# Block-diagonal products of a chunked recurrence over the whole systolic array, two lanes at a time, and attention values two key tiles at a time

## The chip, the cores and the metric

One core of a Trainium2 chip. The metric is the device time of one execution in microseconds (us); the time before is the median of three timed runs, 4041.27 us (4037.69 to 4042.21). A profile is one further execution. PE is the matrix engine (PEld its weight loads), DVE the vector engine, ACT the scalar engine, POOL the general engine, and SP the engine that issues the DMAs spoken of here.

## The reference, cut to what matters

Two trunk layers run over 1024 latent and 256 context tokens of width 1024. Layer 0 mixes the tokens with a bidirectional recurrence over 16 heads, each with a 64 x 64 state; layer 1 with attention of 16 query heads over 4 key and value heads. Each layer ends in a squared-ReLU MLP.

```python
def _wkv_step(state, inp):
    r, w, k, v, kk, bvec = inp
    sa = jnp.einsum('bhvk,bhk->bhv', state, -kk)
    state = state * w[:, :, None, :] + sa[..., None] * bvec[:, :, None, :] + v[..., None] * k[:, :, None, :]
    y = jnp.einsum('bhvk,bhk->bhv', state, r)
    return state, y
...
        sc = jnp.einsum('bqkgd,bskd->bkgqs', q, k_all) * scale
        p = jax.nn.softmax(sc, -1)
        return jnp.einsum('bkgqs,bskd->bqkgd', p, v_all)
```

## The kernel before, in words

The kernel is one program of stages: preparation of the recurrence, the recurrence itself (the chains), its readout and output projection, MLP 0, projections of queries, keys and values, attention, output projection, MLP 1. All in float32; a float32 product is two matmuls in the trace.

**The chains.** The recurrence is cut into chunks of 32 tokens, 40 of them, and runs forwards and backwards at once. Four lanes (`Chain`, one for each four heads: two channel tiles `ct2` by two heads `h`) each make 40 steps; a step serves one chunk in each direction `d`. A step has four stages:

- stage 0 (L859 to L863): eight products give the chunk's right-hand sides, 32 rows each, into `ps_x`, each in a quarter of the array's columns (`tile_position=(0, q)`); ACT copies them to `X`.
- stage 1 (L865 to L874): eight products with the chunk's inverse, again a quarter each, into the other half of `ps_x`; four copies, mostly ACT's, put the result into the stack `SV`. The inverse lies in `T`, for each quarter 32 columns that are zero outside the quarter's own rows; POOL makes it (`inverses`, L843) by multiplying with a mask, one step ahead.
- stage 2 (L879 to L885): eight products with `LS` give the next state, 64 rows for each head, each in a half of the array's columns, into `ps_s`; DVE multiplies by the decay into the next `SV`, twice.
- stage 3 (L887 to L895): eight products give the chunk's outputs, a quarter each, into `ps_y`; ACT copies (first visit of a chunk) or DVE adds (second) to `y`.

`ps_x` has three buffers, `ps_s` and `ps_y` two each. `staggered` (L918) calls the lanes in turn: a round of 16 turns gives each lane its four stages at turns 0, 5, 10 and 11 (`STAGES`), the lanes four turns apart. That is the order in which the instructions are written; a scheduler then places them on the engines by readiness and priority. `Lanes.load` (L800) sends the next two steps' operands, in up to 14 portions of a two-round period (`SENDS`): `ST` (weights of stages 0, 1 and 3), `LS` and the values in `SV`, each send held back until the matmul marked last (`L.mark`) has run. The early and late rounds also carry the first part of the readout (`Readout.center` and `scale`, on DVE, POOL and ACT) beside them.

**The attention** (`phase_e`, L1336). A unit is one head pair and 512 queries; it runs over ten key tiles. For each: four products of full width give the scores `ps_s` (L1404, L1405), ACT takes the exponential into `p`, POOL adds it to `acc` for the sums, and `values` (L1358) multiplies `p` with the value tile, two products of 64 columns each into the two halves of `ps_av`. `values` lags by `AVLAG` = 2 tiles; one tile's values are issued in each iteration. Between them stand products for the next heads' maxima (`ps_m`, L1241), and in the fourth iteration of a unit the sums of the unit before (`ps_su`, L1375), also of 64 columns. `line` ties all of them into one order on PE.

Of the kernel before, what the change touches and what calls it, by code (L numbers as in the profile page):

```python
# [774 lines left out]
class Lanes:  # L775


    def __init__(self, k, es):
        tc, nc = k.tc, k.nc
        sb = lambda n, b: es.enter_context(tc.tile_pool(name=n, reuse_waits="tile", bufs=b))  # L780
        ps = lambda n, b: es.enter_context(tc.tile_pool(name=n, reuse_waits="tile", bufs=b, space=PSUM))
        vp = sb("vp", 1)
        self.gp, self.xp = sb("gp", 2), sb("xp2", 2)
        self.bp = sb("bp", 1)
        self.px, self.pss, self.py = ps("px", 3), ps("pss", 2), ps("py", 2)
        self.SV = [vp.tile([128, 2, 2, 4, 4, 64], F32, name=f"SV{b}", tag=f"SV{b}") for b in range(2)]
        self.LS = [[vp.tile([128, 2, 2, 2, 2, 64, 2], F32, name=f"LS{lp}{b}", tag=f"LS{lp}{b}") for b in range(2)] for lp in range(2)]
        for b, a, h in itertools.product(range(2), range(2), range(2)):
            q = QUAD[a, h] * 32
            (nc.gpsimd if b else nc.vector).memset(self.SV[b][q:q + 32, h, a], 0.0)  # L790
        for h in range(2):
            nc.vector.memset(self.SV[0][h * 64:h * 64 + 64, h, :, 0:4:3], 0.0)
        for t in (self.LS[lp][b] for b in range(2) for lp in range(2)):
            for h in range(2):
                rows = slice(h * 64, h * 64 + 64)
                eye = k.c["ident"][rows, rows].unsqueeze(1).unsqueeze(3).to_broadcast([64, 8, 64, 2])
                nc.scalar.copy(t[rows, h].rearrange("p l d a e c -> p (l d a) e c"), eye)
        self.ST = {}

    def load(self, k, i, mark=None):  # L800

# [8 lines left out]
        for lp in range(2):  # L810
# [4 lines left out]
                yield  # L815
            for h in range(2):
                anti = slice(64 - h * 64, 128 - h * 64)
                send(LS[anti, h].rearrange("p l d a e c -> p (l d a e c)"), S["LS"][h, i, :, :, lp * 2:lp * 2 + 2].rearrange("b s l d a f e -> (b s) (l d a f e)"))
                yield
            for a in range(2) if lp == 0 else ():  # L820
                for h, d in itertools.product(range(2), range(2)):
# [3 lines left out]


class Chain:

# [14 lines left out]
    def step(self, s):  # L845
# [12 lines left out]
        xu = L.px.tile([128, 2, 2, 64], F32, name="ps_x", tag="xu")  # L858
        for ct2, h, d in units:  # L859
            q = QUAD[ct2, h] * 32  # L860
            L.mark = nc.tensor.matmul(xu[q:q + 32, 0, d, :], stack(ct2, h, d, 0), sv(h, ct2, d), start=True, stop=True, tile_position=(0, q))  # L861
        X = L.xp.tile([128, 2, 64], F32, name="X", tag=f"X{pr}")
        L.copied = nc.scalar.copy(X, xu[:, 0])  # L863
        yield
        for ct2, h, d in units:  # L865
            q = QUAD[ct2, h] * 32
            L.mark = nc.tensor.matmul(xu[q:q + 32, 1, d, :], T[:, d, q // 32, :], X[:, d, :], start=True, stop=True, tile_position=(0, q))  # L867
        lo, hi = sorted((2 * gf + c, 2 * gb + 1 - c))
        first = lo not in self.seen
        self.seen |= {lo, hi}  # L870
# [5 lines left out]
        if s + 1 < self.n:  # L876
            self.inverses(s + 1)
            i2, c2 = divmod(s + 1, 2)
            pst = L.pss.tile([128, 2, 2, 64], F32, name="ps_s", tag="s")  # L879
            for ct2, h, d in units:  # L880
                L.mark = nc.tensor.matmul(pst[h * 64:h * 64 + 64, ct2, d, :], ls[:, h, ln, d, ct2, :, c], sv(h, ct2, d), start=True, stop=True, tile_position=(0, h * 64))  # L881
            for h in range(2):
                rows = slice(h * 64, h * 64 + 64)
                pt = k.c["PT"][rows, pr * 2:pr * 2 + 2, :, s + 1].unsqueeze(3).to_broadcast([64, 2, 2, 64])
                nc.vector.tensor_tensor(L.SV[i2 % 2][rows, h, :, both(c2), pr, :], pst[rows], pt, ALU.mult)  # L885
        yield
        psy = L.py.tile([128, 2, 64], F32, name="ps_y", tag="y")  # L887
        for ct2, h, d in units:
            q = QUAD[ct2, h] * 32
            L.mark = nc.tensor.matmul(psy[q:q + 32, d ^ rev, :], stack(ct2, h, d, 32), sv(h, ct2, d), start=True, stop=True, tile_position=(0, q))  # L890
        o = self.y[:, lo:hi + 1:hi - lo, :]
        if first:
            nc.scalar.copy(o, psy)
# [17 lines left out]
                gens.remove(g)  # L911


STAGES = (0, 5, 10, 11)
SENDS = (2, 4, 6, 8, 9, 10, 12, 14, 16, 18, 20, 22, 23, 24)


def staggered(k, L, gens):  # L918


    sends = iter(())
    for t in range(16 * Chain.n + 16):
        i, at = divmod(t, 32)
        if at == 0 and i + 1 < len(Chain.seq):
            sends = L.load(k, i + 1, lambda: L.mark)
        for l, g in enumerate(gens):
            if t >= 4 * l and (t - 4 * l) % 16 in STAGES:
                next(g, None)
        if at in SENDS:
            next(sends, None)  # L930
        yield

# [403 lines left out]
def phase_e(k, outs, qs, qp, mp):  # L1336
# [5 lines left out]
    with ExitStack() as es:  # L1342
# [52 lines left out]
        for i, (ct, half) in enumerate(units):  # L1395
# [4 lines left out]
            for kt in range(10):  # L1400
# [18 lines left out]
                for part in range(2):  # L1419
                    at += 1  # L1420
                    while sent < min(at + MXLEAD, 2 * (at - MX0)):
                        next(mx, None)
                        sent += 1
                    next(post, None)
                    if part == 0 and len(late) > AVLAG:
                        values(*late.popleft())
            done = (ct, half), st
        while late:
            values(*late.popleft())
# [68 lines left out]
```

## Time and profile before

| | |
|---|---|
| median of the timed runs | 4041.27 us |
| the profiled execution's own time | 4029.49 us |
| span of its instructions | 4027.7 us |
| PE busy | 3598.4 us (89%) |
| DVE busy | 2199.1 us (55%) |
| ACT busy | 1507.4 us (37%) |
| POOL busy | 1478.4 us (37%) |
| first and last start of a chain product (L861, L890) | 1013.2, 1417.4 us |
| first and last start of a score product (L1404) | 2747.3, 3184.4 us |

In the rows of a profile, `out<-in` names the tiles, `128*32 128x64` means weights of 128 rows by 32 columns and an operand of 128 partitions by 64 elements. In a timeline, a row has start, duration of the merged group, engine, line and count, and in brackets the engine's idle time before and what ended it; "issue" means that nothing in the profile explains the wait. A matmul's duration overlaps that of its neighbours, so the pace is read from starts.

### The profile page before, as it was taken

The numbers are of one execution on the slowest core, as the hardware profiler recorded it, in microseconds if no ns is written. First come the engines' busy times: TensorE is split into PE (matmuls) and PEld (weight loads), VectorE is DVE, ScalarE is ACT, GpSimd is POOL, SyncE is SP. The second block draws the span as 40 slices with busy tenths as digits, with TensorE's granted clock in tenths as the row PEclk, the third lists the DMA queues.
The fourth block names the chain that finished last, engine by engine and source line by source line (L and its number), as shares of the span: only waits on it lengthen the run. The fifth ranks groups of instructions, "written<-read, shape, count | busy, mean of one in ns | idle before, by whom it ended". The sixth has DMA issues, their size and how long they took to land.

```text
span 4027.7 us, 70776 instructions
## 1 busy us (share of the span) xinstructions
PE 3598.4 (89%) x28100; PEld 2789.5 (69%) x28100; DVE 2199.1 (55%) x3707; ACT 1507.4 (37%) x3223; POOL 1478.4 (37%) x1387
## 2 busy tenths in 40 slices
PE   5999866885677779999999999899999999999998
PEld 3667655664566669788888888765444578888886
DVE  6337789988654784533333335567766453333334
ACT  5666555454455433322111113433444332212222
POOL 3114685665533533111111111135877512222221
PEclk7999965886898789999999999999999999999999
DMA  7456777677777543211111111432010111111111
GB/s 284 144 187 171 171 177 170 160 177 178 198 205 215 163 133 104 80 39 38 42 40 40 38 42 70 138 105 79 17 32 17 63 38 51 47 48 47 50 53 68
DMA packets 397562, 414.77 MB, mean 103 GB/s; under 512 B 152864, under 2 KB 282144, under 8 KB 397104
## 3 DMA queue, kind: packets, MB, share of 16 engines
q1 hardware_dynamic: 396272, 408.94, 36.0%
q8 instruction: 222, 3.64, 0.4%
q0 software_dynamic: 960, 1.31, 0.2%
q14 instruction: 108, 0.88, 0.1%
HBM read 294.99 MB, written 117.11 MB: 102 GB/s over the span
## 4 chain that ended last, share of the span: by engine, by line
PE 66%; DVE 11%; issue 4%; DMA 2%; ACT 1%; POOL 1%; SPq 1%; DVEq 0%; POOLq 0%; ACTq 0%
PE ps_pj L271 45%; PE ps_av L1364 4%; PE ps_s L881 2%; PE ps_m L1241 2%; PE ps_s L1404 2%; PE ps_pj L290 2%; PE ps_s L1405 2%; DVE Tn L713 1%; DVE To L712 1%; PE ps_y L890 1%; PE ps_x L861 1%; PE ps_x L867 1%; DVE sgw L630 1%; DVE KT L653 0%; DVE AR L647 0%
## 5 line engine op out<-in xcount | busy, mean ns | idle before, releaser
L255 POOL TENSOR_TENSOR w_lo<-w_raw,w_hi 128x512 fp32r<-128x512 f32 (+1 forms) x292 | 476.5, 1633 | 1682.5 <-ACT w_hi L253 1635.8
L271 PE MATMUL ps_pj<-xh,w_hi 128*128 128x512 f32 (+1 forms) x1712 | 627.5, 367 | 7.3 <-ACT w_hi L253 5.9
L271 PE MATMUL ps_pj<-xh,w_lo 128*128 128x512 f32 (+1 forms) x1712 | 618.6, 365 | 7.1 <-POOL w_lo L255 7.1
L271 PE MATMUL ps_pj<-xl,w_hi 128*128 128x512 f32 (+1 forms) x1712 | 623.1, 365 | 0.0
L1122 DVE SCALAR_TENSOR_TENSOR xr<-ps_pj,c_mod,xr 128x512 f32<-128x512 f32 (+1 forms) x368 | 251.8, 686 | 564.2 <-PE ps_pj L271 557.4
L253 ACT CAST w_hi<-w_raw 128x512 fp32r<-128x512 f32 (+1 forms) x292 | 216.3, 742 | 836.4 <-PE ps_pj L271 594.6
L271 PE MATMUL ps_pj<-hid_l,w_hi 128*128 128x512 f32 (+1 forms) x1280 | 474.4, 371 | 0.0
L271 PE MATMUL ps_pj<-hid_h,w_hi 128*128 128x512 f32 (+1 forms) x1280 | 473.1, 371 | 0.0
L271 PE MATMUL ps_pj<-hid_h,w_lo 128*128 128x512 f32 (+1 forms) x1280 | 469.8, 370 | 0.0
L1146 DVE TENSOR_TENSOR m_q<-m_r 128x512 f32<-128x512 f32 x160 | 183.8, 1150 | 416.9 <-ACT m_r L1144 416.5
L271 PEld LDWEIGHTS ps_pj<-xh,w_hi 128*128 128x128 f32 x1712 | 325.1, 190 | 62.7 <-ACT w_hi L253 7.9
L271 PEld LDWEIGHTS ps_pj<-xh,w_lo 128*128 128x128 f32 x1712 | 322.9, 190 | 61.2 <-POOL w_lo L255 10.0
L271 PEld LDWEIGHTS ps_pj<-xl,w_hi 128*128 128x128 f32 x1712 | 325.0, 190 | 52.2 <-issue 1.4
L1415 POOL TENSOR_TENSOR acc<-acc,p 128x1024 f32<-128x1024 f32 x122 | 294.8, 2416 | 60.8 <-ACT p L1408 56.6
L271 PEld LDWEIGHTS ps_pj<-hid_h,w_hi 128*128 128x128 f32 x1280 | 241.4, 189 | 44.2
L271 PEld LDWEIGHTS ps_pj<-hid_h,w_lo 128*128 128x128 f32 x1280 | 241.1, 188 | 43.7
L271 PEld LDWEIGHTS ps_pj<-hid_l,w_hi 128*128 128x128 f32 x1280 | 241.4, 189 | 43.3
L1408 ACT ACTIVATE p<-ps_s 128x1024 f32<-128x1024 f32 x160 | 163.5, 1023 | 229.4 <-PE ps_s L1405 229.4
L271 PE MATMUL ps_pj<-xhi,w_hi 128*128 128x512 f32 (+1 forms) x576 | 230.1, 408 | 16.3 <-ACT xhi L479 10.6
L271 PE MATMUL ps_pj<-xlo,w_hi 128*128 128x512 f32 (+1 forms) x576 | 228.2, 397 | 7.4 <-DVE xlo L480 7.2
L1245 DVE TENSOR_REDUCE mc<-ps_m 128x1 f32<-128x512 f32 x256 | 174.8, 690 | 99.8 <-PE ps_m L1241 96.1
L271 PE MATMUL ps_pj<-xhi,w_lo 128*128 128x512 f32 (+1 forms) x576 | 224.1, 391 | 5.5 <-POOL w_lo L255 5.5
(236 smaller groups left out, 6781.0 us busy)
## 6 DMA issues: line engine op xcount, KB each, us to landing
wmod<-in_wmod SPq DMA_DIRECT2D x32, 1024.0 KB
w_raw<-in_m SPq DMA_DIRECT2D x64, 512.0 KB
w_raw<-in_m SPq DMA_DIRECT2D x128, 256.0 KB
ST<-d_ST SPq DMA_DIRECT2D x80, 320.0 KB
d_ST<-AR SPq DMA_DIRECT2D x160, 128.0 KB
d_LS<-KT SPq DMA_DIRECT2D x320, 64.0 KB
d_ST<-G SPq DMA_DIRECT2D x160, 128.0 KB
ST<-d_ST SPq DMA_DIRECT2D x80, 256.0 KB
```

Of the source, the lines that this page charges most:

```text
L253: nc.scalar.copy(hi, raw)
L255: getattr(nc, eng).tensor_tensor(lo, raw, hi.bitcast(F32), ALU.subtract)
L271: i = nc.tensor.matmul(ps[:, :n], w[:, sl], x[:, t0:t0 + n], start=a, stop=z)
L290: nc.tensor.matmul(ps[:, :n], w[:, sl], x[:, t0:t0 + n], start=a, stop=z)
L881: L.mark = nc.tensor.matmul(pst[h * 64:h * 64 + 64, ct2, d, :], ls[:, h, ln, d, ct2, :, c], sv(h, ct2, d), start=True, stop=True, tile_pos ...
L1122: k.nc.vector.scalar_tensor_tensor(x[:, t0:t0 + n], ps[:, :n], g, x[:, t0:t0 + n], ALU.mult, ALU.add)
L1146: nc.vector.tensor_tensor(q[:, :n], r[:, :n], r[:, :n], ALU.mult)
L1241: line(nc.tensor.matmul(ps[:, o:o + n], Q[:, (t + i) * 128:(t + i) * 128 + 128], K_[:, t0:t0 + n], start=True, stop=True))
L1245: line(nc.vector.tensor_reduce(mc[:, t + u, t0 // 512:t0 // 512 + 1], ps, AX.X, ALU.max), "v")
L1364: line(nc.tensor.matmul(st["av"][e * 64:e * 64 + 64], k.V[:, kt, ct // 2 * 64:ct // 2 * 64 + 64], p[:, e], start=(kt == 0), stop=(kt == 9) ...
L1408: nc.scalar.activation(p, ps, AF.Exp)
L1415: (nc.vector if ct == KT - 1 and kt % 3 == 2 else nc.gpsimd).tensor_tensor(st["acc"], st["acc"], p, ALU.add)
```

## The change

In the chains, stage 1 becomes one product for each direction, with all 128 columns of `T` as weights; its blocks outside each quarter's rows are zero. Stage 2 becomes one product for each channel tile and direction over the whole array: weights are both heads' `LS` columns, the operand both heads' stacks, and of the 2 x 2 blocks that come out the two with equal heads are used; `ps_s` doubles to 2 KB a partition. So that both heads' columns lie side by side, `LS` is laid out with the head inside, and its load falls into pieces of 128 elements. The order of calls is now a table, `TURNS`, of stage and lane: lanes 0 and 1 stand together in each stage, and so do lanes 2 and 3, half a round later. `Lanes.line` ties every chain product to the one before it, so PE's order is the written one. In the attention, `values` is called only in odd iterations, then for two key tiles, and ahead of the sums' products instead of behind them.

```diff
+    def line(self, i):
+        if self.mark:
+            self.k.order(i, self.mark)
+        self.mark = i
...
-                send(LS[anti, h].rearrange("p l d a e c -> p (l d a e c)"), S["LS"][h, i, :, :, lp * 2:lp * 2 + 2].rearrange("b s l d a f e -> (b s) (l d a f e)"))
+                send(LS[anti, :, :, :, h].rearrange("p l d a e c -> p (l d a) (e c)"), S["LS"][h, i, :, :, lp * 2:lp * 2 + 2].rearrange("b s l d a f e -> (b s) (l d a) (f e)"))
...
-        for ct2, h, d in units:
-            q = QUAD[ct2, h] * 32
-            L.mark = nc.tensor.matmul(xu[q:q + 32, 1, d, :], T[:, d, q // 32, :], X[:, d, :], start=True, stop=True, tile_position=(0, q))
+        for d in range(2):
+            L.line(nc.tensor.matmul(xu[:, 1, d, :], T[:, d].rearrange("p q j -> p (q j)"), X[:, d, :], start=True, stop=True))
...
-            pst = L.pss.tile([128, 2, 2, 64], F32, name="ps_s", tag="s")
-            for ct2, h, d in units:
-                L.mark = nc.tensor.matmul(pst[h * 64:h * 64 + 64, ct2, d, :], ls[:, h, ln, d, ct2, :, c], sv(h, ct2, d), start=True, stop=True, tile_position=(0, h * 64))
+            pst = L.pss.tile([128, 2, 2, 2, 64], F32, name="ps_s", tag="s")
+            for ct2, d in itertools.product(range(2), range(2)):
+                L.line(nc.tensor.matmul(pst[:, ct2, d], ls[:, ln, d, ct2, :, :, c].rearrange("p h e -> p (h e)"), sv(slice(None), ct2, d), start=True, stop=True))
...
-                nc.vector.tensor_tensor(L.SV[i2 % 2][rows, h, :, both(c2), pr, :], pst[rows], pt, ALU.mult)
+                nc.vector.tensor_tensor(L.SV[i2 % 2][rows, h, :, both(c2), pr, :], pst[rows, :, :, h], pt, ALU.mult)
...
-STAGES = (0, 5, 10, 11)
+TURNS = ((0, 0), (0, 1), (2, 2), (2, 3), (1, 0), (1, 1), (3, 2), (3, 3), (0, 2), (0, 3), (2, 0), (2, 1), (1, 2), (1, 3), (3, 0), (3, 1))
...
-        for l, g in enumerate(gens):
-            if t >= 4 * l and (t - 4 * l) % 16 in STAGES:
-                next(g, None)
-        if at in SENDS:
+        stage, l = TURNS[t % 16]
+        if at[l] % 4 == stage and (l < 2 or t >= 8):
+            next(gens[l], None)
+            at[l] += 1
+        if j in SENDS:
...
+                    if part == 0 and kt % 2:
+                        while len(late) > AVLAG:
+                            values(*late.popleft())
                     next(post, None)
-                    if part == 0 and len(late) > AVLAG:
-                        values(*late.popleft())
```

What stands on the engines, first PE in a middle round of the chains before (`ps_x<-SV` is stage 0, `ps_x<-X` stage 1, `ps_s` stage 2, `ps_y` stage 3; a count is of written products):

```order
L861 MATMUL ps_x<-SV_10268,ST 32x64 x8
L867 MATMUL ps_x<-X,T 32x64 x8
L881 MATMUL ps_s<-SV_10268,LS_10270 64x64 x8
L890 MATMUL ps_y<-SV_10268,ST 32x64 x8
L861 MATMUL ps_x<-SV_10268,ST 32x64 x8
L867 MATMUL ps_x<-X,T 32x64 x8
L881 MATMUL ps_s<-SV_10268,LS_10272 64x64 x8
L890 MATMUL ps_y<-SV_10268,ST 32x64 x8
```

And PE in one round with the change, each row two lanes:

```order
L868 MATMUL ps_x<-SV_10268,ST 32x64 x16
L887 MATMUL ps_s<-SV_10268,LS_10272 128x128 x8
L873 MATMUL ps_x<-X,T 128x64 x4
L896 MATMUL ps_y<-SV_10268,ST 32x64 x16
L868 MATMUL ps_x<-SV_10268,ST 32x64 x16
L887 MATMUL ps_s<-SV_10268,LS_10270 128x128 x8
L873 MATMUL ps_x<-X,T 128x64 x4
L896 MATMUL ps_y<-SV_10268,ST 32x64 x16
```

A lane's step is 22 products for 32, and the shape of the weights changes four times in a round of four lanes, where it changed twice for each lane.

ACT in the late rounds before, without the readout's rows: a copy of stage 0 for one lane, then the four of stage 1 for another.

```order
L863 COPY X<-ps_x 128x128
L874 COPY SV_10269<-ps_x 32x2x64 x4
L863 COPY X<-ps_x 128x128
L874 COPY SV_10269<-ps_x 32x2x64 x4
L863 COPY X<-ps_x 128x128
L874 COPY SV_10269<-ps_x 32x2x64 x4
```

And ACT with the change:

```order
L870 COPY X<-ps_x 128x128 x2
L880 COPY SV_10269<-ps_x 32x2x64 x8
L870 COPY X<-ps_x 128x128 x2
L880 COPY SV_10269<-ps_x 32x2x64 x8
L870 COPY X<-ps_x 128x128 x2
```

The copies now stand in runs of two lanes. PE in the attention before, over two iterations (`ps_s<-Q` and `ps_s<-M` are scores, `ps_m` maxima, `ps_av` values):

```order
L1404 MATMUL ps_s<-Q_28679,K_27203 128x512
L1405 MATMUL ps_s<-M_28680,K_27207 128x512
L1404 MATMUL ps_s<-Q_28684,K_27203 128x512
L1405 MATMUL ps_s<-M_28685,K_27207 128x512
L1241 MATMUL ps_m<-K_27204,Q_29462 128x512
L1364 MATMUL ps_av<-p,Vat 64x512 x2
L1241 MATMUL ps_m<-K_27204,Q_29462 128x512
L1404 MATMUL ps_s<-Q_28679,K_27203 128x512
L1405 MATMUL ps_s<-M_28680,K_27207 128x512
L1404 MATMUL ps_s<-Q_28684,K_27203 128x512
L1405 MATMUL ps_s<-M_28685,K_27207 128x512
L1241 MATMUL ps_m<-K_27204,Q_29462 128x256 x2
```

And with the change:

```order
L1249 MATMUL ps_m<-K_25620,Q_27878 128x512 x2
L1412 MATMUL ps_s<-Q_27486,K_25619 128x512
L1413 MATMUL ps_s<-M_27487,K_25623 128x512
L1412 MATMUL ps_s<-Q_27491,K_25619 128x512
L1413 MATMUL ps_s<-M_27492,K_25623 128x512
L1249 MATMUL ps_m<-K_25620,Q_27878 128x512
L1372 MATMUL ps_av<-p,Vat 64x512 x4
L1383 MATMUL ps_su<-acc,c_ones 64x512 x2
L1249 MATMUL ps_m<-K_25620,Q_27878 128x512
```

Values stand as four products or not at all between two sets of scores, 79 groups where there were 158, and two maxima meet where the values are missing.

More of the change, by code (lines that the diff above doesn't have):

```diff
@@ L796, in __init__ @@
                 eye = k.c["ident"][rows, rows].unsqueeze(1).unsqueeze(3).to_broadcast([64, 8, 64, 2])
-                nc.scalar.copy(t[rows, h].rearrange("p l d a e c -> p (l d a) e c"), eye)
-        self.ST = {}
+                nc.scalar.copy(t[rows, :, :, :, h].rearrange("p l d a e c -> p (l d a) e c"), eye)
+        self.ST, self.k, self.mark = {}, k, None
+    def line(self, i):
+        if self.mark:
+            self.k.order(i, self.mark)
+        self.mark = i
     def load(self, k, i, mark=None):
@@ L860, in step @@
             q = QUAD[ct2, h] * 32
-            L.mark = nc.tensor.matmul(xu[q:q + 32, 0, d, :], stack(ct2, h, d, 0), sv(h, ct2, d), start=True, stop=True, tile_position=(0, q))
+            L.line(nc.tensor.matmul(xu[q:q + 32, 0, d, :], stack(ct2, h, d, 0), sv(h, ct2, d), start=True, stop=True, tile_position=(0, q)))
         X = L.xp.tile([128, 2, 64], F32, name="X", tag=f"X{pr}")
@@ L889, in step @@
             q = QUAD[ct2, h] * 32
-            L.mark = nc.tensor.matmul(psy[q:q + 32, d ^ rev, :], stack(ct2, h, d, 32), sv(h, ct2, d), start=True, stop=True, tile_position=(0, q))
+            L.line(nc.tensor.matmul(psy[q:q + 32, d ^ rev, :], stack(ct2, h, d, 32), sv(h, ct2, d), start=True, stop=True, tile_position=(0, q)))
         o = self.y[:, lo:hi + 1:hi - lo, :]
@@ L911, in side_by_side @@
                 gens.remove(g)
-STAGES = (0, 5, 10, 11)
+TURNS = ((0, 0), (0, 1), (2, 2), (2, 3), (1, 0), (1, 1), (3, 2), (3, 3), (0, 2), (0, 3), (2, 0), (2, 1), (1, 2), (1, 3), (3, 0), (3, 1))
 SENDS = (2, 4, 6, 8, 9, 10, 12, 14, 16, 18, 20, 22, 23, 24)
 def staggered(k, L, gens):
-    sends = iter(())
+    at, sends = [0] * 4, iter(())
     for t in range(16 * Chain.n + 16):
-        i, at = divmod(t, 32)
-        if at == 0 and i + 1 < len(Chain.seq):
+        i, j = divmod(t, 32)
+        if j == 0 and i + 1 < len(Chain.seq):
             sends = L.load(k, i + 1, lambda: L.mark)
-        for l, g in enumerate(gens):
-            if t >= 4 * l and (t - 4 * l) % 16 in STAGES:
-                next(g, None)
-        if at in SENDS:
+        stage, l = TURNS[t % 16]
[3 more added lines that the diff above has]
+        if j in SENDS:
             next(sends, None)
```

## The prediction

> **What bounds the kernel now.** I started from the page: one core, a span of 4027.7 us. The profiled execution took 4029.49 us, so 1.8 us lie around the span; the median of the three timed runs, 4041.27 us, is 11.8 us (0.3%) above it. Terms are worked out against the profiled execution and taken off the median.
>
> ```profile
> span 4027.7 us, 70776 instructions
> ```
>
> The change touches two stages: the chains (about 1013 to 1418 us) and the attention (about 2747 to 3187 us). The windows view gives, for each stretch, its length, then busy time and (x instructions) of PE, PE's weight loads, DVE, ACT and POOL, then the granted clock, and the share and GB/s of the DMA engines.
>
> ```profile
> 1000.00:1013.00 13.00, 0.00 (x0) 0.00 (x0) 11.47 (x16) 6.26 (x6) 12.32 (x17) 0.50 0.89 250
> 1013.00:1050.00 37.00, 26.52 (x728) 21.88 (x730) 30.32 (x64) 12.94 (x56) 21.09 (x38) 0.78 0.62 182
> 1050.00:1300.00 250.00, 186.79 (x6682) 160.48 (x6682) 132.63 (x344) 130.41 (x534) 89.98 (x117) 0.89 0.74 210
> 1300.00:1420.00 120.00, 87.08 (x2784) 71.05 (x2776) 84.75 (x211) 60.08 (x238) 56.83 (x65) 0.82 0.56 155
> 2860.00:2970.00 110.00, 110.00 (x441) 53.59 (x441) 75.72 (x125) 46.37 (x52) 87.18 (x37) 1.00 0.13 30
> ```
>
> In the attention PE is busy for all of the 110 us, so PE bounds it. In the chains PE is busy three quarters of the time at a clock of 0.78 to 0.89, and no other engine is busier except, late, DVE. A step of one lane writes 32 products and the trace holds two matmuls for each, so a round (one step of four lanes) is 256 matmuls: 6682 are 26.1 rounds of 9.58 us, and 2784 are 10.9 rounds of 11.0 us. What PE waits for comes from the view of waits, PE alone, from 1050 to 1300 us (us in total, times, longest):
>
> ```profile
> PE ps_s L881 <- issue: 16.9, 9, 2.5
> PE ps_x L861 <- issue: 16.6, 11, 2.8
> PE ps_y L890 <- issue: 14.4, 11, 2.6
> PE ps_x L867 <- issue: 7.3, 7, 2.0
> PE ps_s L881 <- DVE SV L874: 6.1, 3, 2.9
> ```
>
> 55.2 us go to "issue", in which no semaphore explains the wait, and about 8 to data. The timeline of PE shows where these stops fall:
>
> ```profile
> 1139.66 0.34 PE L881 MATMUL ps_s<-SV,LS 128*64 128x64 f32 x3 [1.88 <-issue]
> 1139.93 0.43 PE L890 MATMUL ps_y<-SV,ST 128*32 128x64 f32 x16
> 1140.18 0.43 PE L861 MATMUL ps_x<-SV,ST 128*32 128x64 f32 x16
> 1140.40 0.43 PE L867 MATMUL ps_x<-X,T 128*32 128x64 f32 x16
> 1140.76 0.70 PE L881 MATMUL ps_s<-SV,LS 128*64 128x64 f32 x16
> 1141.39 0.43 PE L890 MATMUL ps_y<-SV,ST 128*32 128x64 f32 x16
> ...
> 1142.20 0.57 PE L881 MATMUL ps_s<-SV,LS 128*64 128x64 f32 x11
> 1144.33 0.40 PE L881 MATMUL ps_s<-SV,LS 128*64 128x64 f32 x5 [1.56 <-issue]
> ```
>
> Between the two stops stand 3 + 7 x 16 + 11 = 126 recorded matmuls, about 256 instructions with their weight loads, in the middle of a group of like products, where no data can be late. The DMA view of 1050 to 1300 us (packets, MB, share of 16 engines) has a queue that carries instructions:
>
> ```profile
> q1 hardware_dynamic: 24309, 51.41, 72.2%
> q8 instruction: 53, 0.87, 1.5%
> ```
>
> 53 packets of 16 KB in 250 us: one every 4.7 us, two a round, as many as the stops allow. I read this as PE waiting for its next block of instructions, about 1.5 to 2 us of every 4.7. After each stop the clock is lower for a while. So the chains are bound by the number of PE's instructions, not by its arithmetic.
>
> **The chain's products.** Starts of one step in the rows above: outputs 0.25, first products 0.22, inverses 0.36 with the change of shape behind them, states 0.63, together 1.46 us a lane, 5.84 a round. The change leaves the first products and the outputs (16 matmuls each), and makes 16 inverse matmuls into 4 and 16 state matmuls into 8, all with 128x128 weights: 44 for 64 a step, 176 for 256 a round. No row of the stage has this shape. The nearest are the norm's, 20 matmuls of 128x128 weights by 128 columns, each with weights of its own:
>
> ```profile
> 28.83 2.51 PE L356 MATMUL ps_n<-c_ident,n_col 128*128 128x128 f32 x20
> 1607.99 4.64 PE L356 MATMUL ps_n<-c_ident,n_col 128*128 128x128 f32 x20 [1.30 <-DVE n_col L244]
> ```
>
> Less a tail of about 0.3 they go at 0.11 us each with the clock up and 0.21 with it down. I take 0.11, because the long stops that bring the clock down are what goes. Inverses are then 4 x 0.11 = 0.45 and states 8 x 0.11 = 0.90 a lane, for 0.23 without the switch and 0.63: 0.49 more. Switches of array shape fall from eight to four a round; from the attention's rows below I take 0.10 into a narrow shape and 0.26 back, 0.72 a round. PE alone: 4 x (0.25 + 0.22 + 0.45 + 0.90) + 0.72 = 8.0 us a round.
>
> The Trainium skill speaks against this step: "TensorEngine Tiling (Array Packing)", When to Use Tiling, has products of 64 or fewer columns packed side by side, and the change unpacks them. The rows agree on the price (8.0 for 5.84 us of PE); by that rule alone the 40 rounds would be 86 us longer.
>
> **The order of stages.** A round is now two halves of four pairs: first products of one pair of lanes, states of the other, inverses of the first, outputs of the other. The copies behind them, on the same scale:
>
> ```profile
> 1299.92 0.88 DVE L885 TENSOR_TENSOR SV<-ps_s,c_PT 64x256 f32<-64x256 f32 x2 [1.83 <-PE ps_s L881]
> 1300.88 1.10 ACT L874 COPY SV<-ps_x 32x128 f32<-32x128 f32 x4
> ```
>
> With PE counted from the start of a half, a switch at 0.46, states 0.72 to 2.52, inverses to 2.97 and 3.42, outputs to 4.02, the other pair's first products at 4.02 and 4.25. ACT copies from 3.27 (0.3 for PE's tail and the semaphore) to 4.37 and 5.47. There are three buffers for these products, so the second lane of the other pair waits for the first copy, 0.2 us, to 4.45. States of this pair start at 4.94 and 5.84 and need the copies of 4.37 and 5.47: no wait. DVE's 0.88 us twice end at 7.0 and 7.9, a half ends at 4.22, and the next first products are due at 8.44 and 8.66: met, with 1.4 and 0.75 us to spare. A round is 8.45 us. POOL's masks are made two stages ahead and do not end last. All chain products are now tied into one order on PE, so anything late holds every lane; that is why these slacks matter.
>
> A round is 352 instructions, 1.38 blocks. At 8.45 us a round a block lasts 6.1 us, over the 4.7 us in which blocks come now: the stops are covered. If blocks took over 6.1 us they would end last again.
>
> Middle stretch: 26.1 x (9.58 - 8.45) = 29.5 us gained. Late, DVE also serves the readout: 84.75 us of work in 10.9 rounds, 7.8 a round, below 8.45 but with instructions of over 1 us ahead of the state's. The row for PE from 1300 to 1420 us:
>
> ```profile
> PE ps_x L861 <- DVE SV L885: 13.2, 11, 4.0
> ```
>
> is 1.2 us a round. I keep all of it: 9.65 a round, 10.9 x (11.0 - 9.65) = 14.7 gained. The first 37 us wait for loads and for DVE: 0.
>
> **The loads.** The weights of the states now land in pieces of 512 bytes instead of 4 KB, 13.6 MB of the middle's 51.4. The stretch from 330 to 990 us, nearly all packets under 2 KB, bounds them:
>
> ```profile
> DMA packets 243154, 115.08 MB, mean 174 GB/s; under 512 B 112580, under 2 KB 236615, under 8 KB 243086
> q1 hardware_dynamic: 243086, 114.25, 76.0%
> ```
>
> 0.760 x 660 / 114.25 = 4.39 us of all engines a MB against 0.722 x 250 / 51.41 = 3.51: 12 us more at worst, nothing at best. The middle would hold 185 to 197 us of DMA in 220: a share of 0.84 to 0.90, and 0.89 has been reached (1000 to 1013 us). So I cost it at nothing, but it is the next bound, and a round well under 8.45 us would run into it.
>
> **The attention.** Values of two key tiles stand together, so PE leaves and enters the narrow shape half as often: 79 groups for 158. The sums' products already stand beside one values group in each unit, and price the pair:
>
> ```profile
> 2904.54 1.08 PE L1375 MATMUL ps_su<-acc,c_ones 128*64 128x512 f32 x4
> 2905.45 1.03 PE L1364 MATMUL ps_av<-p,Vat 128*64 128x512 f32 x4
> 2906.40 0.50 PE L1241 MATMUL ps_m<-K,Q 128*128 128x512 f32 x1
> ...
> 2908.01 1.08 PE L1364 MATMUL ps_av<-p,Vat 128*64 128x512 f32 x4
> 2909.02 0.50 PE L1241 MATMUL ps_m<-K,Q 128*128 128x512 f32 x1
> 2909.36 0.39 PE L1404 MATMUL ps_s<-Q,K 128*128 128x512 f32 x1
> ...
> 2910.05 0.40 PE L1405 MATMUL ps_s<-M,K 65*128 65x512 f32 x1
> 2910.29 0.40 PE L1241 MATMUL ps_m<-K,Q 128*128 128x512 f32 x1
> 2910.62 0.65 PE L1364 MATMUL ps_av<-p,Vat 128*64 128x512 f32 x2
> ```
>
> Two groups take 1.86, one 1.01: 0.16 less a switch. Before a group the last wide product takes 0.33 to the next start, not 0.24; after it the first takes 0.34: 0.09 and 0.10 more. 0.35 us x 79 = 28 us. Cover: POOL is busy 87.18 of 110 us, DVE 75.72; with 110 shrunk to 103 both still fit. A tile's probabilities are held one iteration longer, and five buffers suffice for that. Ends: 15 if POOL's sums, 2.4 us each, run into the buffers, 30 if not. I take 27.
>
> **Sum**: 29.5 + 14.7 + 27 = 71 us. 4029.5 - 71 = 3958 on the profile's scale, 4041.3 - 71 = 3970 against the median.
>
> **Rivals.** (1) *PE's own pace.* Rounds of 8.0 in the middle and 8.4 late, attention 30: 41 + 28 + 30 = 99, with 0.46 us a round of the switches hidden too 116: 3942 to 3925. For it: PE has hardly any data waits now. Against it: the DMA share of over 0.9 that it needs. 0.12. (2) *Blocks still end last.* With DMA fuller, a block comes every 7 us: 1.38 x 7 = 9.6 a round, the chains gain nothing in the middle and the attention alone stays: 4041 - 27 = 4014; with pieces of 512 bytes at double price (47 us more, 232 / 0.89 = 261 us for the middle) 4025. For it: blocks share the engines with the loads. Against it: their period was 4.7 us at a share of 0.74. 0.14. (3) *Slower: the stops are not the instructions'.* If they belong to each round and stay with the low clock, the wide products are paid on top: 2.6 us x 40 rounds = 104 longer, less 27, 4118. It decides once a round is over 10.8 us, 27 / 40 above the mean of 10.1 now, for then the chains lose the attention's 27. The Trainium skill's "Runtime: NRT & Kernel Launch", Instruction fetch mechanics, would have it so: PE's buffer is said to hold 2048 instructions, refilled in blocks of 256, and crossing a block to be mostly hidden. By that rule the stops stay; the trace agrees on the block of 256 but not that it is hidden, since the stops stand 126 recorded matmuls apart. 0.07.
>
> **How the numbers follow.** The forecast, with the chains gaining 20 to 70 and the attention 20 to 30, has 0.64: 3941 to 4001. The range, 3925 to 4025, takes in rivals 1 and 2 and leaves out 3 and what no rival names (0.03). About 0.2% (8 us) can be told from no change. Faster 0.86: the forecast, rival 1, and 0.10 of rival 2. Same 0.05: the 0.04 of rival 2 in which the chains lose what the attention gains, and 0.01 unnamed. Slower 0.09: rival 3 and 0.02 unnamed.
>
> **What would show it.** Right: PE's waits for "issue" in the chains fall from 55 us to under 15 and the granted clock rises above 0.93; middle rounds last 8 to 9 us; wide products start 0.11 apart; PE starts on the second first product of a pair when a copy ends; 79 values groups in the attention, which is 25 us or so shorter. Wrong: stops again after each 126 or so matmuls (rival 2), first products waiting for DVE or for loads of LS or ST, wide products 0.2 apart, or POOL ending the attention's waits.

## The result, and the profile after

The changed kernel takes 4002.89 us (median of four runs, 3996.86 to 4006.79), the kernel before, on the same chip, 4040.43 (4037.69 to 4042.21): a ratio of 0.9901, 95% interval 0.9889 to 0.9913, so 37.5 us less where 71 were forecast. The profiled execution took 4005.49 us. The windows view of it, for the stretches of the chains (length, busy time and instructions of PE, its weight loads, DVE, ACT and POOL, then clock, DMA share and GB/s):

```profile
1013.00:1050.00 37.00, 26.69 (x408) 24.48 (x408) 27.60 (x57) 9.86 (x43) 21.54 (x38) 0.68 0.59 154
1050.00:1300.00 250.00, 224.82 (x4613) 208.87 (x4613) 130.89 (x348) 121.48 (x538) 87.48 (x116) 0.97 0.83 211
1300.00:1420.00 120.00, 98.81 (x1990) 90.29 (x1988) 84.95 (x214) 59.91 (x245) 57.21 (x67) 0.95 0.68 171
```

A round is 176 matmuls now. In the middle of the chains 4613 of them are 26.2 rounds of 9.54 us: PE is busy for 225 us where it was for 187, the clock is up from 0.89 to 0.97, and a round is no shorter than before (9.58). Late, 1990 are 11.3 rounds of 10.6 us (11.0 before). What PE waits for from 1050 to 1300 us (us in total, times, longest):

```profile
PE ps_x L868 <- ACT SV L880: 25.5, 35, 4.4
PE ps_x L873 <- ACT X L870: 0.8, 1, 0.8
PE ps_x L868 <- DVE SV L891: 0.8, 1, 0.8
PE ps_x L868 <- DMA ST<-d_ST: 0.7, 1, 0.7
```

The 55 us of "issue" are gone, all of them. In their place stands one new row: the first products of a pair's second lane wait for a copy of stage 1, 35 times. The timeline shows one such half-round, in a first visit (start, duration, engine, line; in brackets the idle time before and what ended it):

```profile
1193.50 0.51 DVE L880 COPY SV<-ps_x 32x128 f32<-32x128 f32 x2
...
1193.80 0.41 PE L868 MATMUL ps_x<-SV,ST 128*32 128x64 f32 x16
1193.83 0.79 ACT L880 COPY SV<-ps_x 32x128 f32<-32x128 f32 x3 [2.38 <-DVE SV L880]
...
1194.67 0.43 PE L868 MATMUL ps_x<-SV,ST 128*32 128x64 f32 x16 [0.47 <-ACT SV L880]
...
1195.03 2.15 PE L887 MATMUL ps_s<-SV,LS 128*128 128x128 f32 x16
...
1196.28 1.82 DVE L891 TENSOR_TENSOR SV<-ps_s,c_PT 64x256 f32<-64x256 f32 x4 [2.28 <-PE ps_s L887]
...
1197.02 1.00 PE L873 MATMUL ps_x<-X,T 128*128 128x64 f32 x8
...
1198.13 0.51 DVE L880 COPY SV<-ps_x 32x128 f32<-32x128 f32 x2
...
1198.43 0.41 PE L868 MATMUL ps_x<-SV,ST 128*32 128x64 f32 x16
1198.46 0.79 ACT L880 COPY SV<-ps_x 32x128 f32<-32x128 f32 x3 [2.38 <-DVE SV L880]
```

Read it from the inverses. They start at 1197.02; DVE is then in the middle of four multiplies of the other pair's states, until 1198.10. One of each lane's four stage-1 copies is DVE's, so these start at 1198.13; ACT, idle for 2.38 us until then (the bracket), starts its three at 1198.46. The buffer of the second lane comes free that much later, and every lane stands behind it in the tied order: a half is 1198.43 - 1193.80 = 4.63 us. In the first rounds the copy stands behind longer work of DVE's, transposes of the preparation, and PE waits 4.39 us for it:

```profile
1048.46 1.90 DVE L717 STREAM_TRANSPOSE TTo<-Tn 128x1024 f32<-128x1024 f32 x1
1050.40 0.51 DVE L880 COPY SV<-ps_x 32x128 f32<-32x128 f32 x2
...
1051.65 0.66 PE L868 MATMUL ps_x<-SV,ST 128*32 128x64 f32 x16 [4.39 <-ACT SV L880]
```

In the second visits all four copies are ACT's, since DVE adds to `y` there. The timeline of PE:

```profile
1267.38 0.73 PE L868 MATMUL ps_x<-SV,ST 128*32 128x64 f32 x32
1268.04 2.15 PE L887 MATMUL ps_s<-SV,LS 128*128 128x128 f32 x16
1270.03 1.00 PE L873 MATMUL ps_x<-X,T 128*128 128x64 f32 x8
1270.96 0.65 PE L896 MATMUL ps_y<-SV,ST 128*32 128x64 f32 x32
1271.43 0.73 PE L868 MATMUL ps_x<-SV,ST 128*32 128x64 f32 x32
```

Both lanes' first products run on as one group of 32, and a half is 4.05 us: PE's own pace, 8.1 a round. The sixteen state matmuls take 1.99 us from start to start, 0.117 each with a switch of 0.12.

The DMA view of 1050 to 1300 us (packets, MB, share of 16 engines):

```profile
q1 hardware_dynamic: 49494, 52.12, 82.1%
q8 instruction: 37, 0.61, 1.1%
```

A block of instructions comes every 250 / 37 = 6.8 us instead of 4.7. The loads cost 0.821 x 250 / 52.12 = 3.94 us a MB, for 3.51 before.

In the attention the sums of successive units, in the timeline of PE:

```profile
2874.17 1.03 PE L1383 MATMUL ps_su<-acc,c_ones 128*64 128x512 f32 x4
...
2899.92 1.03 PE L1383 MATMUL ps_su<-acc,c_ones 128*64 128x512 f32 x4
```

A unit is 25.75 us. It was 27.49, from the same rows of before:

```profile
2877.04 1.08 PE L1375 MATMUL ps_su<-acc,c_ones 128*64 128x512 f32 x4
...
2904.54 1.08 PE L1375 MATMUL ps_su<-acc,c_ones 128*64 128x512 f32 x4
```

From the first score to the last it is 412.9 us (2747.7 to 3160.6), for 437.1.

### The profile page after: what moved, and what is told of

Same layout as the page of the kernel before. It is cut to its first block, busy times and chain, and to the rows that moved or that the text cites. A ratio compares the mean times of both kernels' runs of the same rounds, so it can differ in the third digit from the quotient of the medians.

```text
span 4003.7 us, 64456 instructions
## 1 busy us (share of the span) xinstructions
PE 3623.9 (91%) x24932; PEld 2868.4 (72%) x24932; DVE 2186.8 (55%) x3707; ACT 1496.4 (37%) x3223; POOL 1484.7 (37%) x1387
## 4 chain that ended last, share of the span: by engine, by line
PE 63%; DVE 12%; DMA 4%; issue 2%; ACT 2%; POOL 1%; SPq 1%; DVEq 0%; POOLq 0%; ACTq 0%
PE ps_pj L271 45%; PE ps_av L1372 4%; PE ps_s L887 3%; PE ps_m L1249 2%; PE ps_s L1412 2%; PE ps_pj L290 2%; PE ps_s L1413 2%; DVE To L712 1%; DVE Tn L713 1%; DVE SV L891 1%; ACT SV L880 1%; PE ps_x L868 1%; DVE sgw L630 1%; DMA ro_v<-d_V 1%; PE ps_x L873 1%
## 5 line engine op out<-in xcount | busy, mean ns | idle before, releaser
L661 PE MATMUL ps_g<-AR,KB 64*64 64x64 f32 x2560 | 135.1, 266 | 84.5 <-DVE KB L648 60.9
```

The lines of the kernel that those rows point to most:

```text
L661: mm = nc.tensor.matmul(gk[anti, c, :], KB[rows, c].rearrange("p b t -> p (b t)"), AR[rows, c, :], start=True, stop=True, tile_position=(h ...
```

## The experiments

Theory A, from the two traces: the stops were PE waiting for its next 256 instructions, and fewer instructions removed them; what the wide products then should have gained is lost where two lanes' first products share three buffers back to back, because DVE's copy comes late. The rivals: the order removed the stops and not the count; or the loads in pieces of 512 bytes set the pace. The table has every run; "round" is 250 us over the rounds in 1050 to 1300 us (recorded matmuls by the matmuls of a round), "steady" the mean of the 12th to the 25th round alone, from the starts of their first products, "chains" the time from the first to the last start of a chain product, all of the profiled execution; "issue" is the sum of those waits from 1050 to 1300 us.

| run | chain products, order, copies | median us | ratio to before, 95% | round | steady | chains | "issue" |
|---|---|---|---|---|---|---|---|
| before, first profile | narrow, old | 4040.43 | 1 | 9.58 | 9.14 | 404.3 | 55.2 |
| e1, before again | narrow, old | 4045.45, one run | | 9.94 | 9.72 | 413.6 | 59.3 |
| after | wide, pairs | 4002.89 | 0.9901 (0.9889 to 0.9913) | 9.54 | 9.22 | 399.6 | 0 |
| e2, chains alone | wide, pairs | 4023.14 | 0.9956 (0.9939 to 0.9972) | 9.56 | 9.23 | 398.3 | 0.5 |
| e3, attention alone | narrow, old | 4015.32 | 0.9937 (0.9920 to 0.9953) | |  | 411.1 | |
| e4 | wide, pairs, all ACT | 3985.49 | 0.9867 (0.9848 to 0.9887) | 9.09 | 8.70 | 381.4 | 9.3 |
| e5 | narrow, pairs | 4030.49 | 0.9974 (0.9963 to 0.9985) | 9.88 | 9.73 | 420.8 | 51.2 |
| e6 | wide, old | 3987.66 | 0.9872 (0.9854 to 0.9889) | 9.04 | 8.73 | 384.4 | 0 |
| e7, pieces alone | narrow, old | 4044.68 | 1.0009 (0.9998 to 1.0020) | 10.05 | 9.75 | 424.1 | 60.6 |
| e8, inverses alone | inverses wide, old | 4030.02 | 0.9976 (0.9961 to 0.9990) | 9.30 | 8.52 | 406.3 | 14.3 |
| e9 | narrow, old, operand held | 4013.94 | 0.9936 (0.9918 to 0.9953) | 9.10 | 8.73 | 390.9 | 50.8 |
| e10 | e4, operand held | 3961.30 | 0.9804 (0.9790 to 0.9819) | 8.47 | 8.18 | 359.4 | 0 |
| e11 | wide, old, all ACT | 3980.87 | 0.9848 (0.9832 to 0.9865) | 8.98 | 8.72 | 380.9 | 0.5 |

The attention is paired in after, e3 to e6, e10 and e11. The medians of before in the other comparisons were 4039.28, 4040.93 and 4042.47.

**e1 to e3: the parts alone.** e1 is the kernel before once more. 

> The kernel before, profiled a second time. The profiled execution of before took 4029.49 us, its timed runs 4037.69 to 4042.21, and the changed kernel gained 24 us against the first and 38 us against the median of the second. Theory A: how often PE stops for its instructions differs from run to run, so that this profile shows the chains (first product of stage 0 to last of stage 3, 404 us in the first profile) 5 to 15 us longer, the stages behind them unchanged within 2 us. Rival: the 11 us lie in the other stages or around the span, and the chains take 404 us again within 3.

Its chains took 413.6 us, 9.3 more than in the profile that I predicted from; of the 16 us between the two executions 4.9 lie ahead of the chains and 1.7 behind them. The stops differ from run to run, so differences of some 10 us in single profiles of narrow kernels mean nothing.

e2 leaves the attention as it was:

```diff
-                    if part == 0 and kt % 2:
-                        while len(late) > AVLAG:
-                            values(*late.popleft())
...
+                    if part == 0 and len(late) > AVLAG:
+                        values(*late.popleft())
```

> The changed kernel with the attention's values as before, one key tile at a time. Theory A, from the two profiles: the attention gives 23 us of the gain and the chains the rest, so this run takes about 4026 us, 10 to 18 below the kernel before. Rival: the chains gain nothing beyond the noise and the run takes 4035 or more.

e3 makes only this edit of the attention, the other way round, on the kernel before. 

> The kernel before with the attention's values for two key tiles together, the chains untouched. Theory A: 24 groups of narrow products fewer in the middle of each five units at 0.35 us a group, about 1.74 us a unit, in all 20 to 27 us: 4013 to 4020 us. Rival: part of the attention's gain came from what the chains left behind, and this run gains under 15 us.

The chains alone gained 4039.3 - 4023.1 = 16 us, the attention alone 24; together 40, for 37.5 of the whole change. The parts add up, and it is the chains that fell short.

**e4: the copy.** One of four copies goes from DVE to ACT in the changed kernel:

```diff
-                (nc.vector.tensor_copy if first and ct2 == h == 0 else nc.scalar.copy)(SV[q:q + 32, h, ct2, both(c), pr, :], xu[q:q + 32, 1])
+                nc.scalar.copy(SV[q:q + 32, h, ct2, both(c), pr, :], xu[q:q + 32, 1])
```

> The changed kernel with all four copies of stage 1 on ACT, also at the first visit of a chunk, where one of them stood on DVE. Theory A: half a round of first visits takes 4.63 us where one of second visits takes 4.06, because the copy on DVE stands behind 1.82 us of state multiplies and the three on ACT start only after it, so that the buffer for the second lane's first products comes 0.47 us late. Without it half a round of first visits falls to 4.06 to 4.2 us, and 14 to 18 undisturbed rounds gain 12 to 20 us: 3983 to 3991. Rival: at first visits ACT, which copies the outputs as well, is what comes late; with a fourth copy of 0.26 us for each lane on it the wait grows, half a round takes 4.6 to 5.0 us and the time is 4003 to 4015.

It is 17 us faster than after. The timeline, in the same first visits:

```profile
1197.41 1.81 DVE L891 TENSOR_TENSOR SV<-ps_s,c_PT 64x256 f32<-64x256 f32 x4 [3.02 <-PE ps_s L887]
1198.16 1.00 PE L873 MATMUL ps_x<-X,T 128*128 128x64 f32 x8
1198.75 2.15 ACT L880 COPY SV<-ps_x 32x128 f32<-32x128 f32 x8 [2.04 <-PE ps_x L873]
...
1199.56 0.73 PE L868 MATMUL ps_x<-SV,ST 128*32 128x64 f32 x32
...
1203.61 0.73 PE L868 MATMUL ps_x<-SV,ST 128*32 128x64 f32 x32
```

ACT starts 0.59 us after the inverses now, not 1.44; the first products are one group of 32, and a half is 4.05 us. More work for ACT made it faster, since what counted was when the last copy came. But the waits of PE have another row again:

```profile
PE ps_x L868 <- issue: 5.4, 5, 2.5
PE ps_y L896 <- issue: 3.9, 4, 1.1
PE ps_x L868 <- ACT SV L880: 2.7, 4, 1.0
```

At 8.1 us a round a block lasts 5.9 us, the DMA engines are 0.89 busy, and now and then a block is late.

Where in the chains the time lies shows round by round, in us from the first product of the first round named to that of the round behind the last. First visits are rounds 1 to 4 and 9 to 24; the readout's work stands beside rounds 33 to 39; e5, e6 and e8 are explained below.

| run | 1-3 | 4-8 | 9-11 | 12-24 | 25-32 | 33-39 |
|---|---|---|---|---|---|---|
| before | 32.9 | 49.1 | 35.5 | 118.5 | 73.9 | 84.9 |
| after | 42.9 | 42.1 | 38.4 | 120.3 | 70.8 | 76.3 |
| e4 | 33.3 | 46.0 | 32.6 | 113.6 | 71.4 | 75.8 |
| e5, narrow, pairs | 38.5 | 48.5 | 34.0 | 124.5 | 77.0 | 90.4 |
| e6, wide, old order | 36.8 | 45.4 | 33.6 | 113.4 | 70.0 | 76.1 |
| e8, inverses wide | 39.7 | 42.1 | 37.2 | 110.0 | 76.0 | 91.8 |

e1 lies within 1.5 us of before but in 12 to 24, where it takes 126.6. The change loses 10 us in rounds 1 to 3 and 3 in 9 to 11, which the averages of the windows hide. e4 takes its time off the first visits, 9.6, 5.8 and 6.7 us, and gives 3.9 back in rounds 4 to 8. Rounds 33 to 39 are shorter where the products of the states are wide, in either order, and not with the inverses alone (e8). The windows that hold them, before and after:

```profile
1323.00:1409.00 86.00, 61.48 (x1851) 50.10 (x1852) 62.96 (x152) 39.73 (x161) 48.75 (x55) 0.78 0.56 155
1329.00:1406.00 77.00, 64.89 (x1286) 58.85 (x1289) 61.58 (x152) 39.02 (x160) 48.49 (x55) 0.96 0.70 176
```

PE's waits for DVE's multiplies hardly change there, 13.2 us before and 10.5 after; what goes is 7.0 us of "issue", and the clock is up.

**e5 and e6: count or order.** e5 keeps pairs, tied order and layout, but issues every product in narrow groups:

```diff
-        for d in range(2):
-            L.line(nc.tensor.matmul(xu[:, 1, d, :], T[:, d].rearrange("p q j -> p (q j)"), X[:, d, :], start=True, stop=True))
+        for ct2, h, d in units:
+            q = QUAD[ct2, h] * 32
+            L.line(nc.tensor.matmul(xu[q:q + 32, 1, d, :], T[:, d, q // 32, :], X[:, d, :], start=True, stop=True, tile_position=(0, q)))
```

and the states likewise. 

> The changed kernel with its pairs of lanes, its order and its layout of the state, but every product of a round issued as groups of 32 rows and columns, as before: 128 matmuls and 128 weight loads more than e2 has in a round's wide products, so 256 matmuls and 256 loads a round. Theory A (the stops belong to the number of instructions): PE stops again after each 128 matmuls, waits called issue come back at 55 to 75 us in the chains, a middle round takes 9.4 to 9.8 us, the chains 405 to 415 us and the kernel 4010 to 4025 us. Rival (the stops belonged to the order of the stages, and pairing two lanes removed them): no stops, a round at 7.5 us or less, the chains about 320 us, the kernel about 3930 us.

e6 does the reverse: wide products, each lane at its old place, nothing tied:

```diff
-TURNS = ((0, 0), (0, 1), (2, 2), (2, 3), (1, 0), (1, 1), (3, 2), (3, 3), (0, 2), (0, 3), (2, 0), (2, 1), (1, 2), (1, 3), (3, 0), (3, 1))
+STAGES = (0, 5, 10, 11)
...
-            L.line(nc.tensor.matmul(xu[:, 1, d, :], T[:, d].rearrange("p q j -> p (q j)"), X[:, d, :], start=True, stop=True))
+            L.mark = (nc.tensor.matmul(xu[:, 1, d, :], T[:, d].rearrange("p q j -> p (q j)"), X[:, d, :], start=True, stop=True))
```

> The wide products of the changed kernel, but each lane at its own place of a round as before, with no order tied between the two lanes of a pair; the attention in pairs of key tiles. Theory A (the stops go with the instructions, the pair's wait for the product buffer goes with the order): no issue waits, PE busy 4 x 1.82 + 1.44 = 8.7 us a round with the dearer changes between shapes, no wait for the buffer in the first products, a middle round 8.7 to 9.2 us, the chains 375 to 395 us, the kernel 3985 to 4005 us. Rival (pairing is what made the wide products pay): the chains 400 us or more, the kernel 4010 us or more.

The waits of PE in e5, 1050 to 1300 us:

```profile
PE ps_x L868 <- ACT SV L881: 25.8, 29, 4.2
PE ps_x L874 <- issue: 17.4, 14, 2.1
PE ps_y L897 <- issue: 16.8, 12, 2.2
PE ps_s L888 <- issue: 13.1, 11, 2.8
```

Both are there: the stops with the narrow products, the wait for the copy with the pairs. In e6 neither is; the largest row of waits in the stretch has 1.9 us in all, and PE runs nearly without a gap, here one lane and the start of the next:

```profile
1197.16 0.41 PE L868 MATMUL ps_x<-SV,ST 128*32 128x64 f32 x16
1197.50 0.66 PE L873 MATMUL ps_x<-X,T 128*128 128x64 f32 x4
1197.99 1.16 PE L887 MATMUL ps_s<-SV,LS 128*128 128x128 f32 x8
1199.08 0.43 PE L896 MATMUL ps_y<-SV,ST 128*32 128x64 f32 x16
1199.33 0.41 PE L868 MATMUL ps_x<-SV,ST 128*32 128x64 f32 x16
```

2.17 us a lane, 8.67 a round: 0.56 over the pairs' 8.11, which I put down to switching shape for each lane. With e3 and after, the four kernels with the paired attention make a square: narrow products 4015.3 (old order) and 4030.5 (pairs), wide 3987.7 and 4002.9. Wide products gain 27.6 us in either order; pairs cost 15.2 us with either products. Two of these four differences are clean, e5 to after (the products alone) and e6 to after (the order with its ties alone). e3 has the old layout of `LS` as well, so the two differences from it hold the smaller pieces too, which e7 below puts at 4 us, with an interval from -1 to +8. Theory A holds, the rival of the order falls: the pairing of lanes, as the change does it, was not a part of the gain but a loss. The ties were not run apart from the pairs. e6 is where A put it; e5 came out some 6 us above A's times, which had the stops and not this loss.

**e7: the pieces.** The kernel before with only the new layout of `LS`:

```diff
-                send(LS[anti, h].rearrange("p l d a e c -> p (l d a e c)"), S["LS"][h, i, :, :, lp * 2:lp * 2 + 2].rearrange("b s l d a f e -> (b s) (l d a f e)"))
+                send(LS[anti, :, :, :, h].rearrange("p l d a e c -> p (l d a) (e c)"), S["LS"][h, i, :, :, lp * 2:lp * 2 + 2].rearrange("b s l d a f e -> (b s) (l d a) (f e)"))
```

> The kernel before with one thing of the change: the state that the chains load is laid out by lane pairs, so that its loads go in pieces of 512 bytes. Theory A (smaller pieces are dearer, and instruction blocks share the DMA engines with them): the DMA share of the middle chains goes from 0.74 to about 0.80, the blocks of instructions take longer to come, and the kernel is 0 to 10 us longer, 4039 to 4050 us. Rival (the pieces cost nothing, since the loads have time): 4039 us within 4, the same share.

Its window of the middle:

```profile
1050.00:1300.00 250.00, 182.93 (x6368) 156.81 (x6360) 126.93 (x328) 124.85 (x506) 85.89 (x111) 0.88 0.78 201
```

The share rose from 0.74 to 0.78 though fewer bytes moved (201 GB/s for 210), and the time by 4 us, with an interval from -1 to +8 us: both theories' times lie in it. The pieces are dearer; that they cost time here is not shown.

**e8: half of the count.** Only the inverses wide, 208 matmuls a round, on the kernel before:

```diff
-        for ct2, h, d in units:
-            q = QUAD[ct2, h] * 32
-            L.mark = nc.tensor.matmul(xu[q:q + 32, 1, d, :], T[:, d, q // 32, :], X[:, d, :], start=True, stop=True, tile_position=(0, q))
+        for d in range(2):
+            L.mark = nc.tensor.matmul(xu[:, 1, d, :], T[:, d].rearrange("p q j -> p (q j)"), X[:, d, :], start=True, stop=True)
```

> The kernel before with only the products of the inverses over the whole array (the state's products stay narrow, the attention as before): 208 matmuls and as many loads a round in place of 256. Theory A (a round is as long as its blocks of instructions take to come): 416 instructions are 1.63 blocks of 256 at 4.7 us, 7.7 us, with PE busy 7.2 us beside it; a middle round 7.7 to 8.3 us, the chains 320 to 345 us, the kernel 3965 to 3985 us. Rival (other waits, the copies and the state's multiplies, hold the round at about 9): the chains 385 to 400 us, the kernel 4020 to 4035 us.

The time is the rival's, but for neither theory's reason, and the chains' 406 us lie above both forecasts. Where nothing stops it a lane takes 1.81 us, 7.25 a round, as A has it, and issue waits fall from 55 to 14 us. Then the clock goes. The timeline of PE around one stop:

```profile
1270.75 0.41 PE L861 MATMUL ps_x<-SV,ST 128*32 128x64 f32 x16
...
1272.31 0.42 PE L889 MATMUL ps_y<-SV,ST 128*32 128x64 f32 x14
1275.19 0.22 PE L889 MATMUL ps_y<-SV,ST 128*32 128x64 f32 x1 [2.46 <-issue]
```

And the same kernel's windows ahead of the stop and behind it:

```profile
1266.00:1273.00 7.00, 5.95 (x170) 5.03 (x162) 3.87 (x11) 4.23 (x17) 3.35 (x5) 1.00 1.06 248
1275.00:1290.00 15.00, 14.81 (x246) 12.95 (x245) 4.82 (x13) 6.14 (x24) 3.57 (x5) 0.52 0.55 161
1290.00:1296.00 6.00, 6.00 (x106) 5.19 (x104) 2.27 (x6) 2.38 (x10) 1.24 (x3) 0.50 0.71 203
```

One stop of 2.46 us, and for the next 21 us PE works with hardly a pause at half the clock, where a lane takes 3.1 us instead of 1.8. The wide products are the dearer for it. From 1330 to 1370 us, where PE waits for DVE, it is the same at a clock of 0.57 to 0.60. A few stops cost more than their length.

**e9 and e10: the loads out of the way.** `LS` is loaded for the first two steps only and then held:

```diff
-                send(LS[anti, h].rearrange("p l d a e c -> p (l d a e c)"), S["LS"][h, i, :, :, lp * 2:lp * 2 + 2].rearrange("b s l d a f e -> (b s) (l d a f e)"))
+                if i < 2: send(LS[anti, h].rearrange("p l d a e c -> p (l d a e c)"), S["LS"][h, i, :, :, lp * 2:lp * 2 + 2].rearrange("b s l d a f e -> (b s) (l d a f e)"))
```

in the kernel before (e9) and, with its own layout, in e4 (e10). 

> The kernel before, but the second operand of the state's products is loaded for the first two steps only and then held in its buffers, so the chains use stale values and some 45 us of DMA engine time of 155 in the 210 middle us is gone. Theory A (a block of instructions comes late because it shares the DMA engines with these loads): the DMA share of the middle falls from 0.74 to about 0.55, stops in PE shrink from 1.5 us to under 0.8, a middle round takes 8.3 us or less in place of 9.1 to 9.7, and the kernel 4010 to 4026 us. Rival (a block needs its 3 us or so whatever else the DMA engines do): stops as long as before, a round of 9.0 to 9.7 us, the kernel 4035 to 4046 us.

> The kernel of e4 (the changed one with every copy of the first products on ACT), with the second operand of the state's products held after two steps as in e9. Theory A (the stops that came back in e4 are late blocks behind the loads in pieces of 512 bytes): no issue waits in the chains, middle rounds at PE's pace of 8.1 to 8.2 us, the chains 365 to 373 us, the kernel 3965 to 3978 us. Rival (they are a matter of the block and of PE's pace alone): about 9 us of issue waits stay, middle rounds 8.7 us, the kernel 3982 to 3992 us.

The window of the middle of e9:

```profile
1050.00:1300.00 250.00, 191.83 (x7033) 164.37 (x7037) 138.30 (x359) 136.75 (x558) 94.21 (x122) 0.92 0.53 162
```

e9 is 28 us faster, as A gave it, but not as A put it: with the share down to 0.53 there are still 43 stops for 38, of 50.8 / 43 = 1.18 us in the mean for 1.45, and a block comes every 250 / 56 = 4.5 us for 4.7. Most of a block's time is its own, whatever else the DMA engines do; the loads add some tenths of a microsecond. The packets of the instruction queue say the same: from 1050 to 1300 us one takes 1.11 us in the mean in the kernel before and 1.09 in e9, and all 38 stops of the kernel before end 1.2 to 1.7 us after such a packet has ended, with a median of 1.44 us, and 1.42 in e9. A steady round is 8.73 us, between the two forecasts: the time is A's, the stops are rather the rival's. And the window of e10:

```profile
1050.00:1300.00 250.00, 246.10 (x5196) 231.58 (x5196) 131.12 (x323) 154.93 (x670) 100.61 (x133) 0.99 0.58 177
```

Here A holds, with some 4 us more than it gave: no issue waits, PE busy for 246 of 250 us, steady rounds at PE's pace, 8.18 us, and 24 us off e4. At that pace a block lasts 5.9 us in e4 too; only the loads differ. That it is their pieces of 512 bytes, and not the loads as such, e10 can't tell: e9 gained 28 us without loads in pieces of 4 KB.

**e11: the copy in the old order.** The edit of e4 in e6. 

> The kernel of e6 (wide products, each lane at its own place of a round, no order tied) with every copy of the first products on ACT, as e4 does to the changed kernel. Theory A (the copy on DVE costs time only where two lanes' first products share the buffers back to back): no change against e6, middle rounds 8.7 us, the kernel 3982 to 3993 us. Rival (the copy on DVE costs in any order, by delaying DVE's multiplies): 3965 to 3976 us.

It is 7 us faster than e6 with intervals that overlap, 1 us below theory A's times and 5 above the rival's, and its steady rounds are e6's: in these the copy on DVE hurts where pairs share the buffers, not by itself. e4, e6 and e11, at 3985.5, 3987.7 and 3980.9 us, are the versions that compute all of it and beat both kernels; which of them is the fastest these runs don't tell.

## Why the prediction was right and where it was wrong

- **The bound: right.** PE's stops were its instructions. They went to 0 with 352 instructions a round (after, e6), stayed at 51 to 61 us with 512 (e5, e7), and stood at 14 with 416 (e8), and each stop of the kernel before ends 1.2 to 1.7 us after an instruction packet. But the wide products took most of what the stops gave up: PE is busy for 225 of the middle 250 us instead of 187, and a steady round without a stop takes 8.73 us (e6) for 9.14 to 9.72. That the clock is lower after each stop was read wrongly: in the middle stretch of the kernel before it falls to 0.5 within 3.5 us after 8 of the 38 stops and after none of the 21 that are shorter than 1.5 us, and it stays at 1.00 through both stops of the prediction's timeline. The Trainium skill's "Runtime: NRT & Kernel Launch", Instruction fetch mechanics, calls crossing a block mostly hidden. For matmuls as short as these the runs disagree: hidden where a block holds 5.9 us of work and the DMA share is 0.58 (e10), not where it holds some 3 us (5.84 us of products in two blocks, before), even at a share of 0.53 (e9).
- **PE's price: right.** 8.0 us a round was worked out; 8.1 is what PE takes when nothing waits. Wide products start 0.117 apart, for 0.11.
- **The order of stages: wrong, and the step that cost the most.** I let ACT make four copies from 3.27 us of a half on. In the first visits (`first and ct2 == h == 0`) one is DVE's, behind four multiplies that take 1.82 us together, and ACT starts behind it. The wait that I put at 0.2 us made the half 4.63 us instead of 4.22 in the middle, and longer in rounds 1 to 3 and 9 to 11, where work of the preparation or the readout stood ahead of it on DVE too; in the second visits, without DVE's copy, most rounds of the middle took 8.1 to 8.2. e4 undid it: 17 us, with most of the saving in rounds 1 to 3 and 9 to 11. I had worked out when each result was due from a row of the late rounds, all second visits, where ACT makes all four copies.
- **The stretches: 44 us forecast for the chains, 16 gained (e2).** In the profiles of before and after, rounds 1 to 3, about the first 37 us, which I put at nothing, lost 10 us. Rounds 4 to 32, which hold the middle stretch, gained 5 us, or 15 against e1, where 29.5 were forecast. Rounds 33 to 39, most of the late stretch, gained 8.6 for 14.7; PE's wait for DVE, which I kept whole, did stay in the main. e4 brings back 17 of the 28 that are missing.
- **The loads: mis-sized.** 12 us at worst was the bound; at 3.94 for 3.51 us a MB it is 0.43 x 52.12 = 22. The bound came from a stretch of other transfers, at 4.39 us a MB; a packet of 512 bytes took 42.8 ns in the mean (after) and one of 4 KB 253 (before), which is 5.2 us of all engines a MB for 3.9. In the kernel as changed it did not decide, since with the wait for the copy a block had 6.8 us to come; in e4 it is the next bound, as the prediction said of a round well under 8.45: without these loads e10 gains 24 us, though removing a load is more than undoing its pieces.
- **The attention: right.** 0.35 us a group was the price; a unit has five groups fewer and is 1.74 us shorter. 24 us came for 27.
- **Signs and rivals.** Of the signs named, no issue waits, the clock at 0.97 in the middle, wide products 0.117 apart and 79 values groups came; middle rounds of 8 to 9 us came in second visits alone. The time lies 2 us above the forecast's own 3941 to 4001 and near rival 2's 4014, whose mechanism was absent: blocks did not end last. So the range held the time by luck: rival 2 had set its upper end for another reason. The sign of the whole came from the attention (24 us) and from the wide products (27.6); the pairing of lanes took 15.2 back.

## What to carry to other kernels

When an order pairs like stages, look at every engine's queue for the copies that free the shared buffers, in each variant of the loop: an engine that takes one copy in four to relieve another sets the time when it has long work ahead of it. Read "issue" stops that stand a fixed number of instructions apart as a limit on instructions, and test it with the same order at another count, and the same count in another order; a change made of several parts can hold one that loses. And a slack worked out from rows of one phase holds in that phase only.

## What the runs showed of the hardware that was not expected

- After a stop of 2.46 us the granted clock stayed at 0.50 to 0.52 for 21 us of unbroken work of PE (e8). The Trainium skill's "TensorE: Matmul & The Clock Gate", Part 1, has the clock back after one busy window of about 3.4 us; this stretch of packed small products and four wide ones a lane did not bring it back so soon. Why is open.
- Only stops of 1.5 us and more were followed by a lower clock in the middle stretch of the kernel before: 8 of 17, and none of the 21 shorter ones.
- A block of 256 instructions for PE came only every 4.5 us in the mean, with PE waiting for it and the DMA engines half idle (e9). The packet itself took 1.09 us in the mean, and PE went on some 1.4 us after its end.
- With a quarter of the bytes in pieces of 512 bytes instead of 4 KB, the loads held the DMA engines 12% longer a MB (3.94 for 3.51 us).
